# SSD head products of a hybrid decoder, two heads at a time in the two column halves of TensorE's array

## The chip, the cores and the metric

The kernel runs on one core of a Trainium2 chip. The metric is the device time of one execution in microseconds, the median of the runs.

## The reference, cut to what matters

Two layers over 256 tokens of 2048 features: a Mamba-2 SSD mixer and a SwiGLU block, then dilated attention and a second SwiGLU block, all in float32. The change lies in the mixer of the first layer. Its SSD part has 64 heads of 64 channels in 8 groups; the heads of a group share B and C (128 states each).

```python
a_cum = jnp.cumsum(a, axis=-1)
causal = jnp.tril(jnp.ones((SSM_CHUNK, SSM_CHUNK), dtype=bool))
seg = a_cum[..., :, None] - a_cum[..., None, :]
decay = jnp.exp(jnp.where(causal, seg, -jnp.inf))
cb = jnp.einsum('bclgn,bcsgn->bgcls', c, b)
y_diag = jnp.einsum('bgrcls,bcsgrp->bclgrp', decay * cb[:, :, None], x)
...
return (y_diag + y_off).reshape(bsz, seq, n_heads, head_dim).astype(out_dtype)
```

The kernel takes the 256 tokens as two blocks of 128. For each head it forms a masked matrix [source token, target token] of the decays times the C-B product of the group, and multiplies the head's inputs by it: y[target] is the sum over source tokens of x[source] times that matrix.

## The kernel before

All weights stream from HBM as tiles of [128, 2048] float32. Each half tile is split by ScalarE (`wh`, a cast to float32r) and VectorE (`wl`, the rest), and TensorE multiplies with both parts. This weight stream is what TensorE does nearly all the time: in the mixer the lines L238, L239 and L240, each a matmul of a 128x128 stationary part with 256 columns of tokens, into the `acc` banks of PSUM.

Everything else is background: generators in three queues, stepped once behind each half tile (`bg.step()`), as long as the work they issue on VectorE and ScalarE stays within a share of the half tile's time. The order on every engine is the order in which this Python code issues the instructions; there is no scheduler behind it. A matmul of the background thus stands in TensorE's queue between the matmuls of two half tiles. Waits between engines are semaphores that follow from the tiles' readers and writers, and from buffers that are used again.

`ssd(g)` is the background of one group of eight heads. It transposes the inputs, forms the C-B product (`cb`, L535 and L536), masks it into `cbs` (a buffer of 384 columns: source block 0 to both target blocks in columns 0 to 255, source block 1 to target block 1 in 256 to 383), and scales the inputs (`xdt`). Then come ten steps, j = 0 to 9. In step j ScalarE writes the decays of head j into a buffer `ms[j]` (from the pool `wide`, four buffers of 384 columns), VectorE multiplies the decays of head j-1 by `cbs`, and TensorE forms the products of head q = j-2:

- L579: 64 columns of inputs of source block 0, held in the array, with 256 columns of `m`;
- L580: the same for source block 1, with 128 columns of `m`, added to the second half of the first.

A head's output is 64 partitions high. Even heads write partitions 0 to 63 of a bank, odd heads 64 to 127 (`o`, L577); four heads share a bank `yb`. Both operands are float32 and not float32r, and the trace shows each such matmul as two pairs of LDWEIGHTS and MATMUL. The outputs of a group are gated from the ninth step on (`gated`).

`bc_evac(g)` prepares B and C of a group in a tile `bc` of 512 columns, taken from the pool `slots`, whose 28 buffers have 1024 columns each.

Of the kernel before, what the change touches and what calls it, by code (L numbers as in the profile page):

```python
# [16 lines left out]
P = 128  # L17
# [9 lines left out]
class Metered:  # L27
    """An engine whose issued work is summed up, in microseconds."""

# [13 lines left out]
class Background:  # L43
    """Serial queues of generators, stepped behind each piece of the weight stream while the piece's share
    of the vector and scalar engines lasts."""

# [39 lines left out]
def trunk_kernel(  # L86
# [24 lines left out]
    def operand():  # L111
        """Two k-tiles of a transposed activation, each as its float32r part and the exact rest of it."""
        return slot([P, 2, 2, S], F32R)
# [17 lines left out]

# [1 line left out]
    n_tiles = weights.shape[0]  # L133
# [10 lines left out]
    def split():  # L144
        """The next half tile as its float32r part and the exact rest of it."""
        i = state["split"]
        while state["issued"] <= min(i // 2 + 2, n_tiles - 1):
            issue()
        t = raw_tiles[i // 2][:, (i % 2) * 1024:(i % 2 + 1) * 1024]
        h = wpool.tile([P, 1024], F32R, tag="wh", bufs=4, name=name("wh"))  # L150
        l = wpool.tile([P, 1024], F32R, tag="wl", bufs=4, name=name("wl"))
        A.copy(h, t)
        V.tensor_tensor(l, t, h.bitcast(F32), OP.subtract)
        if i % 2:
            del raw_tiles[i // 2]
        ready.append((h, l))
        state["split"] += 1
# [6 lines left out]

# [1 line left out]
    xt = consts.tile([P, 16, S], F32, name="xres")  # L166
# [26 lines left out]

# [1 line left out]
    units = [0]  # L195
# [10 lines left out]
    def n_unit(X, xkey, evac):  # L206
        """[256 tokens, 512 columns] of a product with 2048 features."""
        u = begin_unit(2)
        ps = [acc_bank().rearrange("p a b -> p (a b)") for _ in range(2)]
        for k0 in range(0, 16, 2):  # L210
            h, l = next_half(512)
            bg.need((xkey, k0 // 2))
            for tb in range(2):
                for k in (k0, k0 + 1):
                    xh, xl = (X[k][:, j, tb * P:(tb + 1) * P] for j in range(2))
                    T.matmul(ps[tb], xh, h[:, k % 2, :], start=(k == 0), stop=False)  # L216
                    T.matmul(ps[tb], xh, l[:, k % 2, :], start=False, stop=False)  # L217
                    T.matmul(ps[tb], xl, h[:, k % 2, :], start=False, stop=(k == 15))  # L218
            bg.step()
        bg.add(0, evac(ps, u))  # L220

    def t_units(order, ncols, nk, X, xkey, evacs, q=0):
        """[ncols features, 256 tokens] for every evacuation, two feature tiles a bank; the accumulations
        of several column blocks may take turns."""
        nm = ncols // P
        us = [begin_unit((nm + 1) // 2) for _ in evacs]
        kk = 1024 // ncols
        pss = [[acc_bank() for _ in range((nm + 1) // 2)] for _ in evacs]
        for j, ks in order:
            for k0 in ks[::kk]:  # L230
                h, l = next_half(ncols)
                for k in range(k0, k0 + kk):
                    bg.need((xkey, k // 2))
                    xh, xl = (X[k][:, i, :] for i in range(2))
                    for m in range(nm):
                        o = pss[j][m // 2][:, m % 2, :]
                        wh, wl = (w[:, k % kk, m * P:(m + 1) * P] for w in (h, l))
                        T.matmul(o, wh, xh, start=(k == 0 and m % 2 == 0), stop=False, skip_group_check=True)  # L238
                        T.matmul(o, wh, xl, start=False, stop=False, skip_group_check=True)  # L239
                        T.matmul(o, wl, xh, start=False, stop=(k == nk - 1), skip_group_check=True)  # L240
                bg.step(units[0] == 1)
                if k0 + kk == nk:
                    bg.add(q, evacs[j](pss[j], us[j]))
# [4 lines left out]
    def p_unit(nk, X, xkey, evac):  # L248
        """Two feature tiles of 256 tokens, a bank each: the products with the first part of the
        weights side by side, those with the rest added to the left."""  # L250
        u = begin_unit(2)
# [15 lines left out]

# [1 line left out]
    XT = {}  # L269

    def squares(pair):
        """Adds the squares of two feature tiles to the running sums of all tokens."""
        sq = tmp([P, 2, S])
        A.activation(sq, xt[:, 2 * pair:2 * pair + 2, :], AF.Square)
        G.tensor_tensor(sq[:, 0, :], sq[:, 0, :], sq[:, 1, :], OP.add)  # L275
        pending.append((pair, sq))
# [21 lines left out]
    def token_rstd(sums, rs, scale, eps):  # L298
        """[128, 256] sums of squares over parts of the features -> rs [tokens, 2]."""
        sp = bg_bank()  # L300
        for tb in range(2):
            T.matmul(sp[:, 2 * tb:2 * tb + 2], sums[:, tb * P:(tb + 1) * P], ones[:, 0:2],
                     start=(tb == 0), stop=True, skip_group_check=True)
        yield
        V.tensor_scalar(rs, sp[:, 0:4:2], scale, eps, OP.mult, OP.add)
        G.tensor_tensor(rs, rs, mhalf[:, 0:2], OP.pow)

    def spread(rs):
        """rs [tokens, 2] along the free dimension of every partition, in a bank."""
        dg = tmp([P, 2, P])  # L310
# [56 lines left out]

# [1 line left out]
    def prep():  # L369
# [67 lines left out]
    def first_tap(u, dst, cts):  # L437
        """Taps and bias are halved."""
        for m, ct in enumerate(cts):
# [18 lines left out]
    def bc_evac(g):  # L458
        def gen(ps, u):
            v = scaled(ps[0])  # L460
            bg.done.add(("evac", u))
            yield
            bc, cts = slot([P, 2, S]), (32 + g, 40 + g)
            first_tap(v, bc, cts)
# [7 lines left out]
            gate(bc, th, bc)  # L472
            BC[g] = bc
            yield
# [48 lines left out]
    def ssd(g):  # L523
        bc, xs = BC.pop(g), XS.pop(g)
        ac = {}
# [16 lines left out]
        fetch(1)  # L542
        cbs = wide()
        A.copy(cbs[:, P:S], cb[:, P:S])
# [26 lines left out]
        for j in range(10):  # L571
            if 2 <= j:
                q = j - 2
                m = ms.pop(q)
                if q % 4 == 0:
                    yb[q // 4] = bg_bank()
                o = yb[q // 4][64 * (q % 2):64 * (q % 2) + 64, (q % 4 // 2) * S:(q % 4 // 2 + 1) * S]  # L577
                x0, x1 = (xdt[:, tb, q * 64:(q + 1) * 64] for tb in range(2))
                T.matmul(o[:, 0:256], x0, m[:, 0:256], start=(q % 4 < 2), stop=False, skip_group_check=True)  # L579
                T.matmul(o[:, 128:256], x1, m[:, 256:384], start=False, stop=True, skip_group_check=True)  # L580
            if 1 <= j < 9:
# [57 lines left out]

# [1 line left out]
    H = {}  # L641
# [40 lines left out]

# [1 line left out]
    amask = slot([P, 2, 3, P])  # L684
# [86 lines left out]
    def attend(hf):  # L771
        """Scores, the softmax over the three groups together, and its transpose, for four heads in turn."""
        SB, ST, PB, CB = {}, {}, {}, {}
# [114 lines left out]

# [1 line left out]
OUT0 = [(0, range(0, 28)), (1, range(0, 28)), (0, range(28, 32)), (1, range(28, 32))]  # L890
# [6 lines left out]
def _weights(i):  # L897
    """All weights as tiles of [128 partitions, 2048] in the order of their use: each half of a tile holds
    1024 / n k-tiles of n columns."""
    w_in, w_out = np.asarray(i["ssm_w_in"])[0], np.asarray(i["ssm_w_out"])[0]  # L900
# [4 lines left out]
    def put(ks, *blocks):  # L905
        """blocks: (matrix, first column, columns), side by side."""
        n = sum(b[2] for b in blocks)
# [45 lines left out]
def _constants():  # L953
    """Arrays that depend on the shapes alone: identity, triangles, rotary angles, attention masks."""
    p = np.arange(128)
# [15 lines left out]
def _vectors(i):  # L971
    """The per-feature parameters, one column for every 128 features: mix_norm, ffn_norm, ssm_norm, the convolution's
    taps and bias, D for the two heads of each 128 channels, dt_bias and a_log on both halves of the partitions."""
    cols = [np.asarray(i[n]).reshape(-1, 128).T
# [32 lines left out]
```

## Time and profile before

| | |
|---|---|
| median of 3 runs | 2729.31 us (2729.13 to 2742.91) |
| span of the profiled execution | 2727.3 us |
| TensorE busy (matmuls) | 2708.3 us, 99% |
| VectorE busy | 1705.7 us, 63% |
| ScalarE busy | 1328.7 us, 49% |
| GpSimd busy | 200.9 us, 7% |
| HBM traffic | 181 GB/s over the span |

The profiled execution's own time is its span, first to last instruction; what lies around it is not in the profile. Busy shares are means over stages that do different things, so a stage is read from its own stretch of the trace: the mixer's SSD work stands between about 110 and 600 us. Matmuls are pipelined: the duration of one (0.28 us for 256 columns) is longer than the distance to the next (0.12 us), so in a timeline of TensorE the distance from start to start is what a matmul takes from the queue. PE in the rows is the matmuls, PEld the loads of the stationary operand, which can run beside them.

### The profile page before, as it was taken

To read this page: it belongs to the slowest core of one execution; us is meant where nothing else is said; L and a number is where in the kernel's file an instruction comes from. 1 tells how busy PE (TensorE), PEld (TensorE's weight loads), DVE (VectorE), ACT (ScalarE), POOL (GpSimd) and SP (SyncE) were. 2 spreads that over 40 slices of the span, in tenths; PEclk is the share of its full clock that TensorE was granted. 3 is DMA by queue.
4 is the path that set the end of the run, shared out by engine and by line. 5 is a ranking of instruction groups with operands and counts; after the bars stand their busy time and mean duration, and the time that the engine had idled before them with its cause. 6 is when DMAs were issued, how large, how long until landed. Compare 5 with 4: busy or idle time off the path is not lost.

```text
span 2727.3 us, 41109 instructions
## 1 busy us (share of the span) xinstructions
PE 2708.3 (99%) x16780; PEld 2411.7 (88%) x16780; DVE 1705.7 (63%) x2216; ACT 1328.7 (49%) x2035; POOL 200.9 (7%) x215
## 2 busy tenths in 40 slices
PE   8999999999999999999999999999999999999999
PEld 8999999999988888888888888888988888888888
DVE  6777777755466666665555677776566666665444
ACT  5565555554454444444444454554454444444333
POOL 1012111110000000000000331220000000000000
PEclk9999999999999999999999999999999999999999
DMA  6544444445445555555555554453455555555553
GB/s 229 195 156 163 174 174 171 171 170 182 180 180 186 186 186 187 187 188 190 188 186 199 186 185 167 174 185 139 165 176 194 191 186 194 192 186 194 203 194 135
DMA packets 72588, 495.81 MB, mean 182 GB/s; under 512 B 8448, under 2 KB 10880, under 8 KB 14160
## 3 DMA queue, kind: packets, MB, share of 16 engines
q1 hardware_dynamic: 69552, 483.81, 49.4%
q0 software_dynamic: 2848, 9.37, 1.1%
q8 instruction: 132, 2.16, 0.3%
q14 instruction: 56, 0.46, 0.0%
HBM read 490.99 MB, written 2.16 MB: 181 GB/s over the span
## 4 chain that ended last, share of the span: by engine, by line
PE 98%; DVE 1%; ACT 0%; issue 0%; DMA 0%; SPq 0%; DVEq 0%; ACTq 0%
PE acc L261 36%; PE acc L263 18%; PE acc L238 9%; PE acc L240 8%; PE acc L239 8%; PE acc L218 5%; PE acc L216 5%; PE acc L217 5%; PE bg L579 1%; PE bg L580 1%; PE bg L749 0%; PE bg L782 0%; PE bg L855 0%; DVE wl L38 0%; PE bg L540 0%; DVE slot L38 0%
## 5 line engine op out<-in xcount | busy, mean ns | idle before, releaser
L38 DVE TENSOR_TENSOR wl<-w,wh 128x1024 fp32r<-128x1024 f32 x914 | 1129.6, 1238 | 946.1 <-ACT wh L38 944.5
L38 ACT CAST wh<-w 128x1024 fp32r<-128x1024 f32 x914 | 957.0, 1048 | 1167.4 <-PE acc L261 455.5
L261 PE MATMUL acc<-slot,wh 128*128 128x512 f32 x4096 | 1435.3, 397 | 1.5 <-DVE tmp L38 1.5
L263 PE MATMUL acc<-slot,wl 128*128 128x256 f32 x4096 | 1143.6, 279 | 0.0
L261 PEld LDWEIGHTS acc<-slot,wh 128*128 128x128 f32 x4096 | 769.5, 188 | 187.0 <-PE acc L263 2.1
L263 PEld LDWEIGHTS acc<-slot,wl 128*128 128x128 f32 x4096 | 772.5, 189 | 0.1
L238 PE MATMUL acc<-slot,wh 128*128 128x256 f32 x1936 | 558.5, 288 | 10.3 <-ACT wh L38 10.3
L240 PE MATMUL acc<-slot,wl 128*128 128x256 f32 x1936 | 548.8, 283 | 2.1 <-DVE wl L38 2.1
L239 PE MATMUL acc<-slot,wh 128*128 128x256 f32 x1936 | 548.7, 283 | 0.0
L238 PEld LDWEIGHTS acc<-slot,wh 128*128 128x128 f32 x1936 | 371.7, 192 | 21.4 <-issue 10.8
L240 PEld LDWEIGHTS acc<-slot,wl 128*128 128x128 f32 x1936 | 371.9, 192 | 2.8 <-DVE wl L38 2.8
L239 PEld LDWEIGHTS acc<-slot,wh 128*128 128x128 f32 x1936 | 372.0, 192 | 0.2
L216 PE MATMUL acc<-wh,slot 128*128 128x512 f32 x576 | 229.2, 398 | 0.0
L218 PE MATMUL acc<-wh,slot 128*128 128x512 f32 x576 | 225.0, 391 | 0.0
L217 PE MATMUL acc<-wl,slot 128*128 128x512 f32 x576 | 224.7, 390 | 0.0
L218 PEld LDWEIGHTS acc<-wh,slot 128*128 128x128 f32 x576 | 108.1, 188 | 22.8
L217 PEld LDWEIGHTS acc<-wl,slot 128*128 128x128 f32 x576 | 108.4, 188 | 21.6
L216 PEld LDWEIGHTS acc<-wh,slot 128*128 128x128 f32 x576 | 108.3, 188 | 21.3
L38 ACT ACTIVATE tmp<-tmp 128x256 f32<-128x256 f32 (+1 forms) x104 | 46.8, 450 | 162.7 <-DVE tmp L38 162.7
L275 POOL TENSOR_TENSOR tmp<-tmp 128x256 f32<-128x256 f32 x32 | 27.6, 868 | 1031.7 <-ACT tmp L38 1029.6
L38 DVE TENSOR_TENSOR tmp<-acc,tmp 128x256 f32<-128x256 f32 x176 | 66.1, 417 | 1.3 <-ACT tmp L38 1.3
L38 ACT ACTIVATE wide<-tmp,bias 128x128 f32<-128x128 f32 x192 | 62.9, 391 | 4.8 <-DMA tmp<-acum 4.2
(136 smaller groups left out, 1503.5 us busy)
## 6 DMA issues: line engine op xcount, KB each, us to landing
w<-in_weights_dram SPq DMA_DIRECT2D x455, 1024.0 KB, 4.8
tmp<-acum POOLq DMA_DIRECT2D x32, 256.0 KB, 4.3
xres<-in_x_dram SPq DMA_DIRECT2D x4, 512.0 KB, 8.0
w<-in_weights_dram SPq DMA_DIRECT2D x4, 512.0 KB, 8.6
out_dram<-xres SPq DMA_DIRECT2D x16, 128.0 KB, 1.8
slot<-in_mask_dram POOLq DMA_DIRECT2D x1, 384.0 KB, 5.1
slot<-in_q_norm_dram POOLq DMA_DIRECT2D x1, 192.0 KB, 4.7
slot<-in_k_norm_dram POOLq DMA_DIRECT2D x1, 192.0 KB, 5.2
```

The source lines that it names most:

```text
L38: return call(out, *args, **kw)
L216: T.matmul(ps[tb], xh, h[:, k % 2, :], start=(k == 0), stop=False)
L217: T.matmul(ps[tb], xh, l[:, k % 2, :], start=False, stop=False)
L218: T.matmul(ps[tb], xl, h[:, k % 2, :], start=False, stop=(k == 15))
L238: T.matmul(o, wh, xh, start=(k == 0 and m % 2 == 0), stop=False, skip_group_check=True)
L239: T.matmul(o, wh, xl, start=False, stop=False, skip_group_check=True)
L240: T.matmul(o, wl, xh, start=False, stop=(k == nk - 1), skip_group_check=True)
L261: T.matmul(ps[m], h[:, k % 4, m * P:(m + 1) * P], xk, start=(k == 0), stop=False, skip_group_check=True)
L263: T.matmul(ps[m][:, 0, :], l[:, k % 4, m * P:(m + 1) * P], xk[:, 0, :], start=False, stop=(k == nk - 1), skip_group_check=True)
L275: G.tensor_tensor(sq[:, 0, :], sq[:, 0, :], sq[:, 1, :], OP.add)
L579: T.matmul(o[:, 0:256], x0, m[:, 0:256], start=(q % 4 < 2), stop=False, skip_group_check=True)
L580: T.matmul(o[:, 128:256], x1, m[:, 256:384], start=False, stop=True, skip_group_check=True)
```

## The change

The head products are issued for two heads at a time. In steps j = 3, 5, 7 and 9 TensorE forms the products of heads j-3 and j-2, first both products with source block 0 (the even head, then the odd one), then both with source block 1. The products themselves are the same, as are their outputs' places. Steps 2, 4, 6 and 8 issue none.

The decays of the even head of a pair are held for one step more. The masked C-B product `cbs` no longer takes a buffer of `wide`; it lies in the second half of the tile that holds B and C, which is allocated as 1024 columns instead of 512.

The change also drops docstrings and comments and moves line numbers by one; these hunks are left out.

```diff
@@ bc_evac
-            bc, cts = slot([P, 2, S]), (32 + g, 40 + g)
+            both, cts = slot([P, 1024]), (32 + g, 40 + g)
+            bc = both[:, 0:512].rearrange("p (a t) -> p a t", t=S)
             first_tap(v, bc, cts)
...
-            BC[g] = bc
+            BC[g] = bc, both[:, 512:896]
...
@@ ssd
-        bc, xs = BC.pop(g), XS.pop(g)
+        (bc, cbs), xs = BC.pop(g), XS.pop(g)
...
-        cbs = wide()
         A.copy(cbs[:, P:S], cb[:, P:S])
...
         for j in range(10):
-            if 2 <= j:
-                q = j - 2
-                m = ms.pop(q)
-                if q % 4 == 0:
-                    yb[q // 4] = bg_bank()
-                o = yb[q // 4][64 * (q % 2):64 * (q % 2) + 64, (q % 4 // 2) * S:(q % 4 // 2 + 1) * S]
-                x0, x1 = (xdt[:, tb, q * 64:(q + 1) * 64] for tb in range(2))
-                T.matmul(o[:, 0:256], x0, m[:, 0:256], start=(q % 4 < 2), stop=False, skip_group_check=True)
-                T.matmul(o[:, 128:256], x1, m[:, 256:384], start=False, stop=True, skip_group_check=True)
+            if j >= 3 and j % 2:
+                pair = (j - 3, j - 2)
+                mm = [ms.pop(q) for q in pair]
+                if pair[0] % 4 == 0:
+                    yb[pair[0] // 4] = bg_bank()
+                for tb in range(2):
+                    for q, m in zip(pair, mm):
+                        o = yb[q // 4][64 * (q % 2):64 * (q % 2) + 64, (q % 4 // 2) * S:(q % 4 // 2 + 1) * S]
+                        T.matmul(o[:, tb * P:], xdt[:, tb, q * 64:(q + 1) * 64], m[:, 256 * tb:256 + 128 * tb],
+                                 start=(tb == 0 and q % 4 < 2), stop=(tb == 1), skip_group_check=True)
             if 1 <= j < 9:
                 V.tensor_tensor(ms[j - 1], ms[j - 1], cbs, OP.mult)
```

On TensorE, at the first head products of the first group, the order before is this (`acc` is the weight stream's bank, `bg` the background's, `wide` the masked decays of the head, the `slot` of L579 and L580 the inputs `xdt`; the size is that of the output):

```order
L238 MATMUL acc_1339<-slot_106,wh_1266 128x256
L239 MATMUL acc_1339<-slot_106,wh_1266 128x256
L240 MATMUL acc_1339<-slot_106,wl_1267 128x256
L579 MATMUL bg_1413<-wide_1333,slot_1300 64x256
L580 MATMUL bg_1413<-wide_1333,slot_1300 64x128
L238 MATMUL acc_1338<-slot_148,wh_1305 128x256
L239 MATMUL acc_1338<-slot_148,wh_1305 128x256
L240 MATMUL acc_1338<-slot_148,wl_1306 128x256
```

One head's two products stand between two half tiles; those of the second head follow one half tile of 24 stream matmuls later. After the change nothing stands at the first place, and at the second this:

```order
L238 MATMUL acc_1338<-slot_148,wh_1304 128x256
L239 MATMUL acc_1338<-slot_148,wh_1304 128x256
L240 MATMUL acc_1338<-slot_148,wl_1305 128x256
L580 MATMUL bg_1452<-wide_1332,slot_1299 64x256
L580 MATMUL bg_1452<-wide_1371,slot_1299 64x256
L580 MATMUL bg_1452<-wide_1332,slot_1299 64x128
L580 MATMUL bg_1452<-wide_1371,slot_1299 64x128
L238 MATMUL acc_1337<-slot_153,wh_1339 128x256
L239 MATMUL acc_1337<-slot_153,wh_1339 128x256
```

The products of the first head moved one half tile back, to those of the second, and the four alternate between the heads, from `wide_1332` to `wide_1371` and again.

On VectorE, in the same steps, the masking and the first mask product stand as follows before (`wl` is the weight stream's):

```order
L38 TENSOR_TENSOR wide_1296<-bg_1253,cm 128x128 x2
L38 TENSOR_TENSOR slot_1300<-bg_1256,dtn 128x512
L38 TENSOR_TENSOR slot_1300<-bg_1257,dtn 128x512
L38 TENSOR_TENSOR wl_1306<-w_1145,wh_1305 128x1024
L38 TENSOR_TENSOR wl_1341<-w_1145,wh_1340 128x1024
L38 TENSOR_TENSOR tmp_1369<-acc_1041,rb 128x512
L38 TENSOR_TENSOR wide_1333<-wide_1333,wide_1296 128x384
```

and after:

```order
L38 TENSOR_TENSOR slot_594<-bg_1253,cm 128x128 x2
L38 TENSOR_TENSOR slot_1299<-bg_1256,dtn 128x512
L38 TENSOR_TENSOR slot_1299<-bg_1257,dtn 128x512
L38 TENSOR_TENSOR wl_1305<-w_1145,wh_1304 128x1024
L38 TENSOR_TENSOR wl_1340<-w_1145,wh_1339 128x1024
L38 TENSOR_TENSOR tmp_1368<-acc_1041,rb 128x512
L38 TENSOR_TENSOR wide_1332<-wide_1332,slot_594 128x384
```

The sequence is the same; the masked product is written to and read from `slot_594`, the tile of B and C, instead of `wide_1296`.

## Rows read from the trace of the kernel before

**Rows 1.** The page: span, busy time, chain that ended last.

```profile
span 2727.3 us, 41109 instructions
...
PE 2708.3 (99%) x16780; PEld 2411.7 (88%) x16780; DVE 1705.7 (63%) x2216; ACT 1328.7 (49%) x2035; POOL 200.9 (7%) x215
...
PE 98%; DVE 1%; ACT 0%; issue 0%; DMA 0%; SPq 0%; DVEq 0%; ACTq 0%
PE acc L261 36%; PE acc L263 18%; PE acc L238 9%; PE acc L240 8%; PE acc L239 8%; PE acc L218 5%; PE acc L216 5%; PE acc L217 5%; PE bg L579 1%; PE bg L580 1%; PE bg L749 0%; PE bg L782 0%; PE bg L855 0%; DVE wl L38 0%; PE bg L540 0%; DVE slot L38 0%
```

**Rows 2.** Busy time by stretch: the SSD stretch (columns in the first line).

```profile
core 0: us, PE busy (x) PEld busy (x) DVE busy (x) ACT busy (x) POOL busy (x), PEclk, DMA share, GB/s
110.00:600.00 490.00, 488.77 (x3799) 458.00 (x3797) 347.27 (x507) 292.18 (x508) 74.73 (x83) 1.00 0.48 170
```

**Rows 3.** Groups by line: shapes, count | busy us, mean ns | idle before.

```profile
L579 PE MATMUL bg<-wide,slot 128*64 128x256 f32 x128 | 41.3, 405 | 0.0
L580 PE MATMUL bg<-wide,slot 128*64 128x128 f32 x128 | 24.4, 273 | 0.0
```

**Rows 4.** Lines L579 and L580 alone: durations min/median/max, waits before and behind.

```profile
L579 PE MATMUL bg<-wide,slot x128: 378/404/431, 122.4 to 596.7; 128*64 128x256 f32 x128
...
  issue: 0.7, 2
...
L580 PE MATMUL bg<-wide,slot x128: 272/273/273, 122.9 to 597.1; 128*64 128x128 f32 x128
...
  ACT wide L38: 0.6, 2
```

**Rows 5.** Timeline of PE around the first head: start us, duration us, instruction.

```profile
122.23 0.28 PE L240 MATMUL acc<-slot,wl 128*128 128x256 f32 x1
122.44 0.43 PE L579 MATMUL bg<-wide,slot 128*64 128x256 f32 x1
...
122.70 0.38 PE L579 MATMUL bg<-wide,slot 128*64 128x256 f32 x1
...
122.92 0.27 PE L580 MATMUL bg<-wide,slot 128*64 128x128 f32 x1
...
123.03 0.27 PE L580 MATMUL bg<-wide,slot 128*64 128x128 f32 x1
123.23 0.39 PE L238 MATMUL acc<-slot,wh 128*128 128x256 f32 x1
123.45 0.28 PE L239 MATMUL acc<-slot,wh 128*128 128x256 f32 x1
```

**Rows 6.** Timeline of PEld (weight loads), the same stretch.

```profile
122.43 0.13 PEld L579 LDWEIGHTS bg<-wide,slot 128*64 128x64 f32 x1
...
122.49 0.14 PEld L579 LDWEIGHTS bg<-wide,slot 128*64 128x64 f32 x1
...
122.70 0.14 PEld L580 LDWEIGHTS bg<-wide,slot 128*64 128x64 f32 x1
...
123.23 0.19 PEld L238 LDWEIGHTS acc<-slot,wh 128*128 128x128 f32 x1 [0.17 <-issue]
```

**Rows 7.** Timeline of PE and PEld around a float32 product of full width.

```profile
354.05 0.28 PE L240 MATMUL acc<-slot,wl 128*128 128x256 f32 x1
354.17 0.59 PE L315 MATMUL bg<-tmp,ones 128*128 128x256 f32 x2
...
354.71 0.28 PE L239 MATMUL acc<-slot,wh 128*128 128x256 f32 x1
...
354.05 0.31 PEld L315 LDWEIGHTS bg<-tmp,ones 128*128 128x128 f32 x2
```

**Rows 8.** Timelines: DVE's mask product of the second head, and that head's products on PE.

```profile
122.37 0.55 DVE L38 TENSOR_TENSOR wide<-wide,wide 128x384 f32<-128x384 f32 x1
...
126.29 0.65 PE L579 MATMUL bg<-wide,slot 128*64 128x256 f32 x2
```

## The prediction

> **What bounds the kernel now.** I read the page first: TensorE (PE) is busy for 99% of the span and the chain that ended last runs through it for 98%; the chain gives the two head-product lines, L579 and L580, 1% each [rows 1]. Next the stretch in which the SSD mixer runs, 110 to 600 us: PE 488.8 of 490 us, VectorE (DVE) 347, ScalarE (ACT) 292, the DMA engines at 0.48 of their time, PE's granted clock 1.00 [rows 2]. So a microsecond taken off PE's queue there comes off the end, as long as the other engines keep up, and they have 143 and 198 us to spare. Because PE's matmuls are pipelined, "busy" says little about what one costs: L579 and L580 together count 41.3 + 24.4 us busy [rows 3]. What a pair of head products takes from the weight stream is read from starts in the timeline instead.
>
> In the weight stream one matmul of 256 columns follows the next after 0.12 us [rows 5]. Take the stretch around one head's two products, a "visit". The last stream matmul before it starts at 122.23, the second one after it at 123.45: 1.22 us, of which two steps of 0.12 belong to the stream itself. The visit costs 0.98 us. Each product appears as two matmuls (x128 for 64 heads, [rows 3]): it is float32 and goes through the array in two passes. The starts 122.44, 122.70, 122.92, 123.03 and 123.23 split the cost:
> - streaming: 0.22 + 0.22 us for the product of 256 columns, 0.11 + 0.11 for that of 128, 0.66 in all;
> - the change over to a 64-column array: the last stream matmul is through at 122.35, the first weight load of the visit starts at 122.43 to 122.44, 0.09 us; that load is uncovered, since the first pass takes 0.26 instead of 0.22: 0.04;
> - the change back: the last pass is through at 123.14, the next load starts at 123.23 [rows 5, 6]: 0.09; and that stream matmul takes 0.22 instead of 0.12: 0.10.
>
> So 0.66 us stream and 0.32 us changing over. That the 0.32 is the price of the narrower array, and not of any visit, is seen where a float32 product of full width (L315, 256 columns) stands in the same stream: from 354.05 to 354.71 is 0.66 us, less 0.24 is 0.42, just two passes of 0.21, with its load started early [rows 7]. Within a visit the loads are covered: the second load starts at 122.49 and its pass follows when the first is through [rows 5, 6]. All 128 instances of each line lie within a few per cent of one duration [rows 4], and nothing waits: the lines have 0.7 us of idle time before them in total. 64 visits of 0.98 are 62.7 us, 2.3% of the span.
>
> **The change, part by part.** *Two heads in one visit.* 64 visits become 32 with the same matmuls; each saves one changeover, 0.32 us, if nothing else happens. The two heads go to different column halves of the array (outputs on partitions 0 to 63 and 64 to 127), in the order A (256 columns), B (256), A (128), B (128). Whether two halves stream at the same time is what no row shows, since in the trace heads never stand next to each other. The bounds come from the visit: nothing overlaps, 1.32 us of streaming for two heads; or everything does, 0.66. In between lies what the order of issue allows, and this is what I take. Passes start in the order of the queue, and a load starts when the matmul ahead of it starts (122.70 in both views, [rows 5, 6]). From the first load: A's passes 0.04 to 0.26 and 0.26 to 0.48; B's first load is issued at 0.26, its passes run 0.30 to 0.52 and 0.52 to 0.74; A's second product, issued at 0.52, runs 0.56 to 0.67 and 0.67 to 0.78; B's second must wait for B's half, 0.74 to 0.85 and 0.85 to 0.96. With the changeovers (0.09 ahead, 0.19 behind) the visit takes 1.24 us, against 1.96 for two visits now. 32 times 0.72 is **23.0 us**. If loads are pulled ahead further, A's second pass and B's first run together and the end comes at 0.92: 1.20 us, 24.3 us saved.
>
> *What waits.* A pair needs DVE's mask product of its second head. For the first pair that ends at 122.92 and the visit of that head starts at 126.29, 3.4 us later [rows 8]; with head A's visit gone it would start 0.98 earlier, still 2.4 us of cover. Head A's scores are kept one step longer; that needs a fourth buffer of `wide`, and that is the one that the masked C-B product leaves. ACT, which writes these buffers, waited on L580 for 0.6 us in all [rows 4]; freed in pairs they may come later for every second head, by one visit, and ACT's 198 idle us cover 32 times 1.24 = 40 us. Cost 0, at most a few us.
>
> *The masked C-B product in the B/C tile.* Same instructions, same sizes; only where they read differs, 0.55 us for each mask product [rows 8]. The tile was of slot size already, and is now held some eight steps longer. The order of DVE, ACT, GpSimd and SyncE keeps every instruction at its place, so no queue is passed. Even 0.1 us more on each of 64 products would lie in DVE's 143 idle us. Cost 0.
>
> **Rivals.** *The halves do not stream together, but the change between them is free*: the change does not do what its words say. The visit takes 0.04 + 1.32 + 0.28 = 1.64 us, 32 times 0.32 = 10.2 us saved, 2719.1. For it: the trace has no two matmuls of PE streaming at once. If moreover the three loads that go to the other half are uncovered, 0.04 each, 0.20 us remain: 6.4 us, 2722.9. The second load of L579 speaks against that; it starts at 122.49 in the middle of a pass on the same rows [rows 5, 6]. The Trainium skill, "TensorE: Matmul & The Clock Gate", Part 3 (the mechanism) states that a load runs over a matmul in flight only where the row group differs, and two column halves share their rows; by that rule it would be 2722.9. The trace does not agree for one half (that load starts at 122.49); for two no run shows it.
>
> *Everything overlaps*: a pair costs as much as one head now, 0.98, and 32 times 0.98 = 31.4 us go, 2697.9. It needs B's first pass to start with A's first, though A's second stands ahead of it in the queue and needs A's half; I see no row for it. The Trainium skill, in the same Part 3 (measured speedup), gives tiles in different columns starts about 4 ns apart and 2.38 times for three of them; by that alone this rival is the outcome. No run here shows it.
>
> *Changing the half costs what changing the width costs.* Then the three changes within a visit (A to B, B to A, A to B) pay 0.09 + 0.04 each as on the way in: 1.64 + 0.39 = 2.03 us against 1.96, 32 times 0.07 = 2.2 us **slower**, 2731.5; at the price of the way out, 0.19 each, 2.21 us, 8.0 us slower, 2737.3. It decides from 0.32 / 3 = 0.107 us a change. For it: the rows show 0.09 whenever the array is set to other columns. Against it: what changes there is the width, which stays here. The Trainium skill, "TensorEngine Tiling (Array Packing)", Key Properties, has a drain for a change of mode and none for another tile of it; by that rule this rival falls. No run shows it yet.
>
> **How the numbers follow.** The sum is made against the span, 2727.3 us [rows 1]; the median of the runs is 2729.3, and the 2.0 us around the span stay. 2729.3 - 23.0 = 2706.3, 24.3 gives 2705.0; I say **2706**. Chances: partial overlap 0.60; full overlap 0.06; no overlap and free changes 0.14, with uncovered loads 0.06; half changes that drain 0.09; something not seen here, such as a buffer freed late that holds up ACT and through it the split weights, 0.05. The range reaches from full overlap, 2697.5, to no overlap, 2720, and leaves out the last three, 0.20. A measurement can tell 0.5%, 13.6 us, from no change: both overlaps are faster by more, 0.66 and a little of the unseen, **0.67**; the rivals without overlap and the draining one lie within it, **0.29** with a share of the unseen; **0.04** slower by more.
>
> **What would show it.** In the changed profile's timeline, the head products (now one line, L580) stand in eights. Right: from the first load to the change back about 0.95 us, B's first pass starting under 0.1 us after A's second, and the stream's 0.12 steps broken for 1.24 us. Starts that step 0.22, 0.22, 0.22, 0.22, 0.11 and so on, each behind the last: no overlap, 1.64. Gaps of 0.09 or more between one half and the other: the draining rival. Idle time of PE ahead of L580 released by DVE, or ahead of L238 to L240 released by ACT: a wait that I costed at nothing. Elsewhere nothing should move, since only layer 0's mixer issues these lines.

## The result and the profile after

The changed kernel took 2711.74 us (median) against 2729.28 us before; the ratio is 0.9898, with a 95% interval of 0.9852 to 0.9945. In a second set of runs it was 2698.15 against 2729.32, ratio 0.9886 (0.9856 to 0.9917). One run of the changed kernel, 13427.01 us, and one of the kernel before, 3300.41 us at a granted clock of 0.753, stand far off all others, no run shows why, and they are left out below.

These medians can't be understood without one fact that the runs brought out. In the two SwiGLU blocks the weight stream is pairs of matmuls, L261 (512 columns) and L263 (256), and each block runs at one of two paces, 0.353 or 0.347 us a pair, taken up anew in each execution, by either kernel. A block at the longer pace (a long block, in short) costs about 13.4 us more. So the times of both kernels fall on three levels, for none, one or both blocks at the longer pace; a profiled execution shows which blocks were long, for the other runs it is read from the time. Over all runs of both kernels:

| both short | one long | both long | |
|---|---|---|---|
| 2715.9 (10 runs) | 2729.3 (16) | 2742.8 (13) | before |
| 2685.1 (2) | 2698.3 (5) | 2711.7 (2) | changed |
| 30.8 | 31.0 | 31.1 | difference |

On equal levels the change is worth **31 us**, 1.1%. The first median shows 17.5 us because it compares two levels: one long block before, two after.

In the page of the changed kernel, TensorE is still what bounds, as in [rows 1]:

```profile
span 2710.0 us, 41100 instructions
...
PE 2690.8 (99%) x16780; PEld 2402.5 (89%) x16780; DVE 1705.2 (63%) x2216; ACT 1327.7 (49%) x2035; POOL 202.3 (7%) x215
...
PE 98%; DVE 1%; ACT 0%; DMA 0%; issue 0%; SPq 0%; DVEq 0%; ACTq 0%
```

The timeline of PE around the first pair of heads (start us, duration us; the eight matmuls of a visit stand merged in one row) answers to [rows 5]:

```profile
125.22 0.28 PE L239 MATMUL acc<-slot,wh 128*128 128x256 f32 x1
125.34 0.28 PE L240 MATMUL acc<-slot,wl 128*128 128x256 f32 x1
125.55 0.87 PE L580 MATMUL bg<-wide,slot 128*64 128x256 f32 x8
126.35 0.39 PE L238 MATMUL acc<-slot,wh 128*128 128x256 f32 x1
126.58 0.28 PE L239 MATMUL acc<-slot,wh 128*128 128x256 f32 x1
```

From 125.34 to 126.58 is 1.24 us, less two steps of 0.12 is 1.00 for two heads, where one head cost 0.98. All visits within the stream agree: 0.992 to 0.993 us in this trace, 0.985 to 0.987 in that of the kernel before. Narrower windows on the same stretch show how the eight stand together:

```profile
125.55 0.44 PE L580 MATMUL bg<-wide,slot 128*64 128x256 f32 x2
...
125.82 0.39 PE L580 MATMUL bg<-wide,slot 128*64 128x256 f32 x2
...
126.14 0.28 PE L580 MATMUL bg<-wide,slot 128*64 128x128 f32 x2
```

They start in twos, and two last 0.44 us together where one lasted 0.43 [rows 5]; the two starts of each couple lie 6 or 7 ns apart in the trace. So the first pass of the odd head starts with the first pass of the even one. The loads are not held back either: the odd head's first load starts 5 ns into the even head's first pass, and all eight loads of the visit stand beside its passes:

```profile
125.55 0.63 PEld L580 LDWEIGHTS bg<-wide,slot 128*64 128x64 f32 x8
```

The line's own view answers to [rows 4]:

```profile
L580 PE MATMUL bg<-wide,slot x256: 272/326/430, 125.6 to 566.3; 128*64 128x256 f32 x64, 128*64 128x128 f32 x64
...
  issue: 0.3, 1
...
  ACT wide L38: 0.3, 1
```

The last head product starts at 566.3 instead of 597.1, 30.8 us earlier, and TensorE waits for nothing that it had not waited for before. From there to the wait in the second SwiGLU block the stream is 30.7 us ahead of the kernel before. The rest happens in that block. This view counts the L261 matmuls in 200 us of the first and of the second SwiGLU block (window, its length, PE busy with their count, PEld likewise, granted clock, DMA share, GB/s). Before:

```profile
1100.00:1300.00 200.00, 200.00 (x567) 106.45 (x567) 1.00 0.52 186
2200.00:2400.00 200.00, 200.00 (x578) 108.28 (x577) 1.00 0.53 190
```

Changed:

```profile
1100.00:1300.00 200.00, 200.00 (x567) 106.37 (x567) 1.00 0.52 187
2200.00:2400.00 200.00, 200.00 (x567) 106.36 (x567) 1.00 0.52 186
```

567 in 200 us is 0.353 us for an L261 and the L263 behind it, 578 is 0.346; from start to start the trace has 0.3533 and 0.3467. The profiled execution of before had its second block at the shorter pace, that of the changed kernel had not, at the same granted clock; over 698 us of stream the 1.9% make 13.4 us, the gap between 30.7 and the 17.3 us by which the spans differ.

### The profile page after: what moved, and what is told of

The parts are those of the page before. It is cut to its first block, busy times and chain, and to the rows that moved or that the text cites. A ratio compares the mean times of both kernels' runs of the same rounds, so it can differ in the third digit from the quotient of the medians.

```text
span 2710.0 us, 41100 instructions
## 1 busy us (share of the span) xinstructions
PE 2690.8 (99%) x16780; PEld 2402.5 (89%) x16780; DVE 1705.2 (63%) x2216; ACT 1327.7 (49%) x2035; POOL 202.3 (7%) x215
## 4 chain that ended last, share of the span: by engine, by line
PE 98%; DVE 1%; ACT 0%; DMA 0%; issue 0%; SPq 0%; DVEq 0%; ACTq 0%
PE acc L261 36%; PE acc L263 18%; PE acc L238 9%; PE acc L240 8%; PE acc L239 8%; PE acc L218 5%; PE acc L216 5%; PE acc L217 5%; PE bg L580 1%; PE bg L750 0%; PE bg L783 0%; PE bg L856 0%; DVE wl L38 0%; PE bg L541 0%; DVE slot L38 0%; ACT wh L38 0%
## 5 line engine op out<-in xcount | busy, mean ns | idle before, releaser
L261 PE MATMUL acc<-slot,wh 128*128 128x512 f32 x4096 | 1448.3, 399 | 1.5 <-DVE tmp L38 1.5
L263 PE MATMUL acc<-slot,wl 128*128 128x256 f32 x4096 | 1150.2, 281 | 0.0
L261 PEld LDWEIGHTS acc<-slot,wh 128*128 128x128 f32 x4096 | 769.6, 188 | 193.5 <-PE acc L263 2.1
L263 PEld LDWEIGHTS acc<-slot,wl 128*128 128x128 f32 x4096 | 773.7, 189 | 0.1
```

What stands on the lines that cost most here:

```text
L261: T.matmul(ps[m], h[:, k % 4, m * P:(m + 1) * P], xk, start=(k == 0), stop=False, skip_group_check=True)
L263: T.matmul(ps[m][:, 0, :], l[:, k % 4, m * P:(m + 1) * P], xk[:, 0, :], start=False, stop=(k == nk - 1), skip_group_check=True)
```

## Experiments

**The changed kernel again**, more runs of it and of the kernel before on one chip.

> The changed kernel once more, beside the kernel before. What is at stake: in its profile the mixer ended 30.7 us earlier than before, but the end came only 17.3 us earlier; the 13.4 us were given back after 2025 us (before) and 1994 us (after), in the second SwiGLU block, where a pair of stream matmuls (L261, L263) took 0.3467 us before and 0.3534 after. Theory: that is a state which each execution takes up anew when TensorE restarts after its last wait of that block, whatever the kernel; then both kernels' times fall into two levels about 13.4 us apart (near 2729 and 2743 before, near 2698.5 and 2712 after), and on equal levels the change is worth 30.5 us. Rival: the change itself brings the slower level, then all its runs lie near 2712 and those of before near 2729, 17 us.

Measured: 2698.39, 2698.19, 2698.25, 2698.11, 2685.18 and 2685.00 us; the kernel before beside it 2729.3 to 2729.5 seven times and 2715.8 to 2715.9 four times. The theory holds, and the rival falls, since the changed kernel has the shorter levels, too. There is one addition: both blocks draw, so there is a third level 13.4 us lower, and the three were complete once the kernel before showed 2742.6 to 2743.1 on other chips. How often which pace comes up differs from chip to chip: on one, eight of nine runs of the kernel before had both blocks long, on another five of eight had both short. In the profiled execution of this set the first block was long and the second short (567 and 578).

**Both heads of a pair in the same half.**

```diff
-                        o = yb[q // 4][64 * (q % 2):64 * (q % 2) + 64, (q % 4 // 2) * S:(q % 4 // 2 + 1) * S]
+                        o = yb[q // 4][64 * (q % 4 // 2):64 * (q % 4 // 2) + 64, (q % 2) * S:(q % 2 + 1) * S]
...
-                                 start=(tb == 0 and q % 4 < 2), stop=(tb == 1), skip_group_check=True)
+                                 start=(tb == 0 and q % 2 == 0), stop=(tb == 1), skip_group_check=True)
```

> The changed kernel, but both heads of a pair go to the same column half (heads 0 and 1 to partitions 0 to 63 of a bank, heads 2 and 3 to 64 to 127); the outputs of heads 1 and 2 thereby change places. Theory that the gain is the two halves streaming at once: a visit takes 1.64 us instead of 0.99 (one changeover of 0.32 saved of two, the streams one after another), so the mixer ends 32 x 0.65 = 20.8 us later than with the change. Rival, that the gain is fewer visits and something other than the halves: it stays at 0.99 us.

The timeline of PE, same place:

```profile
125.35 0.28 PE L240 MATMUL acc<-slot,wl 128*128 128x256 f32 x1
125.56 1.51 PE L580 MATMUL bg<-wide,slot 128*64 128x256 f32 x8
127.00 0.39 PE L238 MATMUL acc<-slot,wh 128*128 128x256 f32 x1
127.23 0.28 PE L239 MATMUL acc<-slot,wh 128*128 128x256 f32 x1
```

127.23 - 125.35 - 0.24 = 1.64 us a visit, the number expected, and 0.64 more than with two halves. The run took 2719.28 us, with one block long, 21.0 us above the changed kernel at that level (2698.3) and 10.0 below before (2729.3). So of the 31 us, 10 come from half as many changeovers and 21 from the two halves streaming at once.

**The order A, A, B, B.**

```diff
-                for tb in range(2):
-                    for q, m in zip(pair, mm):
+                for q, m in zip(pair, mm):
+                    for tb in range(2):
```

> The changed kernel with the four products of a visit in the order A (256 columns), A (128), B (256), B (128) in place of A, B, A, B. Theory 1, each half has a queue of its own and takes its matmuls whatever stands ahead of them for the other half: B's first pass again starts with A's first, the visit stays at 0.99 us. Theory 2, matmuls start in the order of the program (as the prediction had it): B's first pass starts with A's last at the earliest, 0.55 us after the first, and the visit takes 0.32 + 0.55 + 0.66 = 1.53 us, 32 x 0.54 = 17 us more than the change.

The timeline of PE:

```profile
125.68 0.28 PE L240 MATMUL acc<-slot,wl 128*128 128x256 f32 x1
125.89 0.88 PE L580 MATMUL bg<-wide,slot 128*64 128x256 f32 x8
126.70 0.39 PE L238 MATMUL acc<-slot,wh 128*128 128x256 f32 x1
126.92 0.28 PE L239 MATMUL acc<-slot,wh 128*128 128x256 f32 x1
```

126.92 - 125.68 - 0.24 = 1.00 us: theory 1. All four passes of A stand ahead of B's first in the program, yet the second matmul of the visit starts 13 ns after the first. It must be B's: the row does not name the half, but passes of one half follow each other after 0.22 us, or 0.11 with 128 columns, as the same-half run shows. Each half takes its own matmuls without waiting for those of the other half ahead of them; the order within a visit hardly matters. The run took 2685.53 us, with both blocks at the shorter pace.

**The tile alone.** The kernel before with only the masked product moved.

```diff
-            bc, cts = slot([P, 2, S]), (32 + g, 40 + g)
+            both, cts = slot([P, 1024]), (32 + g, 40 + g)
...
-        cbs = wide()
```

> The kernel before with only the masked C-B product moved into the tile of B and C; one head a visit as before. Theory: nothing changes, visits of 0.98 us, the last head product at 597 us as before within 0.5 us, DVE's mask product 0.55 us. Rival, that the move carries part of the gain or costs something: a mask product that is not 0.55 us, or a mixer that ends at another time.

The head products and DVE's mask products of this kernel:

```profile
L579 PE MATMUL bg<-wide,slot x128: 379/404/430, 123.1 to 597.4; 128*64 128x256 f32 x128
...
120.16 0.55 DVE L38 TENSOR_TENSOR wide<-wide,slot 128x384 f32<-128x384 f32 x1
```

The visits take 0.99 us, as before; a mask product takes 0.55. The last of L579 starts at 597.4 where before had 596.7 [rows 4], but the first is 0.7 us later too, 123.1 against 122.4. The move costs and brings nothing by itself. Its 2716.27 us is not a gain: both blocks ran at the shorter pace, at which the kernel before takes 2715.9.

**What sets the pace.** Three steps, none of which settles it wholly. A block begins with 44 units of 32 pairs each. In the 14 traces of this study both blocks begin at the longer pace. Behind the 48th pair stands L302, four matmuls of full width with 2 columns, and in 27 of the 28 blocks the pace turns to the shorter one there; the 28th, in the same-half run, had turned by itself at its 27th pair. The pace that a block then keeps to its end, if nothing more is put in, is taken up where TensorE waits for VectorE behind the third unit; this is that wait in the kernel before, second block (the bracket is the idle time and what ended it):

```profile
2023.22 0.28 PE L263 MATMUL acc<-slot,wl 128*128 128x256 f32 x1
2024.25 0.47 PE L261 MATMUL acc<-slot,wh 128*128 128x512 f32 x1 [0.75 <-DVE tmp L38]
```

First, a useless matmul in each of the 44 units of both blocks, narrow in one kernel, of full width in the other (in `swiglu`, behind the first `yield`):

```diff
+            T.matmul(bg_bank()[0:64, 0:2], ones[:, 0:64], ones[:, 0:2], start=True, stop=True, skip_group_check=True)
```
```diff
+            T.matmul(bg_bank()[:, 0:2], ones, ones[:, 0:2], start=True, stop=True, skip_group_check=True)
```

> The changed kernel with one matmul of no use more in each of the 44 units of both SwiGLU blocks: 64 columns of ones held, 2 columns streamed, so that the array changes to the narrow form and back once a unit. It puts 88 restarts of another kind into the stretch where a pair of stream matmuls takes either 0.3534 or 0.3467 us. Theory 1, any interruption of TensorE's stream draws the level anew: units at either level, in a mixed order, some 30 to 60 of 88 fast. Theory 2, only a wait for another engine draws it (as at the third unit of each block): the level set there stays, all units after it alike. Theory 3, the interruption's form decides: all units after an interruption at one level, in both blocks. If that is the fast one, an interruption (about 0.35 us) once a block would be worth 13.4 us wherever the level was slow.

> The same with the useless matmul at full width (128 columns held, 2 streamed), so that nothing changes over. The products of this form that stand in each block ahead of the third unit (L302) left the level as it was in every trace so far. Theories 2: the level stays what the wait at the third unit made it. Theory 1: mixed. Theory 3: one level, which may differ from that of the narrow form.

Measured: 2746.88 and 2722.93 us. With the narrow one all units behind the wait ran at the longer pace, 0.3532 us a pair between the useless matmuls, each of which costs 0.40 us. With the wide one the units alternated, 0.3467 and 0.3533, 20 of each in either block. That the interruption's form decides (theory 3) fits the narrow kernel; the wide one's alternation no theory had, except that it excludes a lasting level (theory 2) and a draw at random (theory 1). The expectation was wrong in one point: it says that L302 left the level as it was, but L302 had turned it in every trace.

Second, one narrow matmul a block behind the wait (`if j == 6`), then also one wide (`if j == 8`):

> The changed kernel with one useless narrow matmul (64 columns held, 2 streamed) in each SwiGLU block, behind the seventh unit, after the last wait. With such a matmul in every unit all units ran at the slow level. Theory: the wait at the third unit draws the level, each block and execution anew, and a narrow matmul behind it sets it to slow: every run alike, both blocks at 0.3533 us a pair, near 2711.8 + 2 x 0.35 = 2712.5, no run near 2699 or 2685. Rival: the level comes from something else that varies between executions (the position of data, the clock's phase): then the runs spread over the three levels as before.

> The same, and two units later one useless full-width matmul in each block. In every unit such matmuls made the level alternate, unit by unit, in both blocks. Theory: the narrow one sets slow, the wide one turns it to fast: every run with both blocks at 0.3467 us a pair from there on. Against the changed kernel with both blocks slow, 2711.8, less about 2 x 13 us and plus 2 x 0.6 us for the matmuls and the slow units ahead of them: near 2686.5, every run. Rival as above: runs at several levels.

> Four heads a visit, and the narrow and the wide matmul in each SwiGLU block. Theory: 5 us below the two-head kernel with the same two matmuls, near 2682, every run; against the kernel before, whose runs spread over 2716, 2729 and 2743, a ratio near 0.982. Rival: the levels return, runs at several levels.

Measured: 2712.08 to 2712.88 us; 2712.98 to 2713.24; 2707.65 to 2708.68. The wide matmul did not turn the pace. These are the first and the second block of the two-head kernel with both matmuls (two_fast):

```profile
1100.00:1300.00 200.00, 200.00 (x567) 106.37 (x567) 1.00 0.52 188
2200.00:2400.00 200.00, 200.00 (x567) 106.36 (x566) 1.00 0.51 184
```

The kernel with the narrow matmul alone shows little: on this chip the kernel before had both blocks long in eight of nine runs without any such matmul.

Third, the same with the wide matmul three units behind the narrow one (`j == 9`). At the longer pace the starts repeat every three pairs: from an L261 to its L263 it is 0.241, then 0.236, then 0.232 us. The count of pairs from the start of such a pattern tells at which of the three places the wide matmul comes:

> As two_fast, with the wide matmul one unit later: three units (96 pairs) behind the narrow one instead of two (64). At the slow level the starts repeat every three pairs (0.241, 0.236, 0.232 us for L261). In the kernel with a wide matmul in every unit the level turned from slow to fast where 24 pairs, a multiple of three, had passed since the slow pattern began anew with 0.241, and stayed slow after 16; in two_fast it was 64, no multiple of three, and it stayed slow in all runs. Theory: the place in the pattern of three decides, 96 is a multiple, so both blocks run at 0.3467 us a pair from there on, every run near 2713.1 - 2 x 12.3 = 2688.5. Rival: the level after the wide matmul has nothing to do with the count; then 2713 again or a mixture.

> The same with four heads a visit: 4.5 us less, near 2684, every run, by the theory; 2708.5 or a mixture by the rival.

Measured: 2686.02 to 2689.76 and 2682.31 to 2684.18 us; by these times every run had both blocks short at the end. The two blocks of the kernel with four heads a visit:

```profile
1100.00:1300.00 200.00, 200.00 (x578) 108.16 (x578) 1.00 0.53 190
2200.00:2400.00 200.00, 200.00 (x578) 108.16 (x578) 1.00 0.53 190
```

In the traces of these two, all four blocks were short before the narrow matmul. Three stayed so through both matmuls, which refutes that a narrow one sets the longer pace. The fourth fell to the longer pace at the narrow one and turned back at the wide one, as the count says. By itself that is one turned block, and on this chip the kernel before, too, had both blocks short in five of eight runs. Two runs of the two-head kernel took 3.1 to 3.7 us more than the other two, about what two blocks lose that are long from the wait to the wide matmul (an estimate: 2 x 240 pairs of 6.6 ns, 3.2 us); they have no profile that would show it.

But the traces of all runs together show what a wide matmul does to a block at the longer pace. At 76 places such matmuls, L302 or the useless ones, come behind a pair of the longer pace. Where the L261 ahead had taken 0.235 or 0.236 us to its L263, the pace turned to the shorter one, 66 times of 66. Behind the two other places of the pattern, 0.232 to 0.233 and 0.240 to 0.241 us, it stayed, 10 times of 10; the wide matmuls of the second step stood there, at 0.232. So in these traces the place in the pattern decides. Why it does is not shown, and the wide matmul is no cure: at the shorter pace it turned a block to the longer one 41 times of 44. What the wait ends in is not explained by the place: all 26 waits that came behind a step of 0.230 or 0.231 us left 15 blocks long and 11 short.

**Four heads a visit.**

```diff
-            if j >= 3 and j % 2:
-                pair = (j - 3, j - 2)
+            if j in (5, 9):
+                pair = range(j - 5, j - 1)
...
+        ms, extra = {}, slot([P, 1024])
...
-                m = ms[j] = wide()
+                m = ms[j] = extra[:, 512 * (j - 3):512 * (j - 3) + 384] if j in (3, 4) else wide()
```

> The changed kernel with four heads a visit, in steps 5 and 9: A, B, A, B with 256 columns, then A, B, A, B with 128; two of the buffers that hold decays come from a further tile of `slots`. Theory, halves stream side by side and a visit costs one changeover: 0.33 + 2 x 0.66 = 1.65 us in place of two visits of 0.99, 16 x 0.33 = 5.3 us less than with two heads a visit, at equal levels of the two SwiGLU blocks (near 2706.4, 2693.0 or 2679.7). Rival: a buffer that comes free late makes ScalarE wait and TensorE after it; then TensorE shows waits ahead of L238 to L240 in the mixer that the two-head kernel does not have, and the gain is smaller or turns.

Measured: three runs at 2707.1 to 2707.2 us and one at 2694.01, 4.6 and 4.2 us below the two-head kernel at the same levels, where 5.3 had been expected; ratio to before, whose runs lay on all three levels, 0.987 (0.983 to 0.991). The timeline of PE (the sixteen matmuls of a visit between these rows):

```profile
133.92 0.28 PE L240 MATMUL acc<-slot,wl 128*128 128x256 f32 x1
...
135.58 0.39 PE L238 MATMUL acc<-slot,wh 128*128 128x256 f32 x1
135.80 0.28 PE L239 MATMUL acc<-slot,wh 128*128 128x256 f32 x1
```

135.80 - 133.92 - 0.24 = 1.64 us, as expected. One new wait takes a part of the gain back, TensorE for GpSimd ahead of a product of full width (waits of PE: total, times, longest):

```profile
PE bg L315 <- POOL tmp L312: 0.4, 1, 0.4
```

With the two useless matmuls behind the wait (four_fast_b) this is the quickest kernel of the study: 2682.49 us beside 2716.15 before, ratio 0.9865 (0.9841 to 0.9889). A part of that ratio is the levels, of which these runs of before had two. With both blocks short the kernel before takes 2715.9 and the two-head kernel 2685.1, and it beats both.

## Why the prediction came out as it did

The direction was right and the median, 2711.74, lies in the range of 2697.5 to 2720. But the number, 2706, was reached by a mechanism that did not happen, and that the median came out 5.7 us from it is luck: with one block long, the level of the 2729.3 that the sum started from, the changed kernel takes 2698.3, and a second long block, which the prediction did not know of, put 13.4 us on top.

*What bounds* was right: 0.98 us a visit, made of 0.66 streaming and 0.32 changing over, and all of what a visit loses comes off the end. The same-half run gives the rival without overlap to 0.01 us, 1.64, so this split and the price of a changeover stand. One reading of [rows 4] was loose: L579 does not have one duration but two, 0.43 us for a first pass and 0.38 for a second; nothing hangs on it.

*Partial overlap, 1.24 us a visit*, was the step that failed. It took the order of the queue to bind across halves: B's first pass behind A's second. The trace has B's first pass 6 to 7 ns behind A's first, and 13 ns with three of A's passes between them in the program. What happened is the rival of full overlap, which was given 0.06: 0.98 a pair and 31.4 us, measured 1.00 and 31. I had read "a load starts when the matmul ahead of it starts" from loads of one half and carried it to two, where the odd head's first load starts 5 ns into the even head's first pass. The Trainium skill, in "TensorE: Matmul & The Clock Gate", Part 3 (measured speedup), adds about 4 ns to the span for each further tile, and has tiles in different columns within about 5 ns of tiles in different rows. These runs agree, with the two of a couple 6 to 7 ns apart, and it should have weighed more. In the same Part 3 (the mechanism) the Trainium skill also has it that a load overlaps with a matmul in flight only in another row group. That does not hold for two column halves here: with loads of the second half uncovered the visit could not take 1.00 us.

*What waits* and *the tile* at no cost were right: 0.3 us of waiting on L580, and the tile alone changed nothing. *Half changes that drain* did not occur: a visit takes 1.00 us where that rival had 2.03. The Trainium skill, in "TensorEngine Tiling (Array Packing)", Key Properties, has a drain for a change of the tiling mode and not for a change of the tile alone. The 1.00 us agrees.

*"Elsewhere nothing should move"* failed, though not by the change. The two SwiGLU blocks were read from one execution as if they had one time; the mean of 397 ns that the profile gives for L261 hid that the two blocks of that trace ran at 0.353 and 0.347. The three runs shown of before held the hint, two at 2729 and one at 2742.91. So a gain of 31 us stands as 17.5 in one set of medians and as 31.2 in the other, and the bound of 0.5% for what a measurement can tell was too low: two sets of runs at different levels differ by 13.4 or 26.9 us with no change at all.

## What to carry to other kernels

Here two matmuls of 64 columns cost what one costs, 0.99 us a visit, if they go to different column halves of the array (outputs on partitions 0 to 63 and 64 to 127 of PSUM) and stand in one visit, float32 in two passes included. What a narrow visit costs beyond its streaming is the change to the narrow array and back, 0.32 us, so narrow products are collected. Before a price of under a per cent is believed, the trace is compared with that of before instruction by instruction along the whole program: a constant lead that shrinks in a stretch without changed code is not the change.

## What the hardware showed that I had not expected

- The two column halves run ahead of each other: B's first pass 13 ns behind A's first with A's other three passes ahead of it in the program.
- A stream of 128x128 loads with 512 and 256 columns by turns has two paces at the same granted clock of 1.00, 0.353 and 0.347 us a pair. The longer one repeats its starts every three pairs, the shorter one every two or every one; each holds for hundreds of us, with one exception until something interrupts the stream. A full-width matmul of 2 columns turned the longer into the shorter at one of the three places, 66 times of 66, and at the others never, 0 of 10. Why the wait behind the third unit ends in one or the other is open.
- Setting the array to 64 columns and back costs 0.32 to 0.34 us around any such visit, whether 4, 8 or 16 matmuls stand in it: 0.98, 1.00 and 1.64 us, less 0.66, 0.66 and 1.32 of streaming.
